# The last expert's down projection in two column halves, each scaled and scattered by itself

## The chip, the cores and the metric

The kernel runs on one core of a Trainium2 chip. The metric is the device time of one execution in microseconds (us), the median of several runs. The engines named here are PE (TensorE, matrix products), DVE (VectorE), ACT (ScalarE), POOL (GpSimd, which also issues the indirect transfers) and SP (SyncE, which issues all other transfers of this stage). Each engine takes its own instructions strictly in the order in which they stand in its queue; an instruction that waits holds up everything behind it on that engine.

## The reference, cut to what matters

The layer ends in a mixture of 16 experts. Each expert picks its 128 best tokens of 1024, computes a SwiGLU block on them and adds the result, times a gate, to the tokens' rows:

```python
gate, idx = lax.top_k(jnp.swapaxes(aff, 1, 2), cap)            # cap = 128
xg = h[bidx, idx]
hid = jax.nn.silu(xg @ w_e_gate) * (xg @ w_e_up)
y = (hid @ w_e_down) * gate[..., None]
out = jnp.zeros_like(h).at[bidx, idx].add(y)                   # then x_new + mod_l[5] * out
```

All matrices of an expert are 1024 x 1024 in float32. The 16 experts run from about 1193 us to the end.

## The kernel before, in words

A product in float32 is made of three products of shorter numbers: every operand is split into a high part (`h`, cast by ACT, line 94) and a low part (`l`, the difference, made by DVE, line 95), and `mm3` (lines 98 to 100) issues high x high, high x low and low x high into one PSUM sum. For the weights the parts are named `eh` (3 buffers) and `el` (2 buffers), each 128 x 2048, made by `split_raw` from a raw tile of 1 MB (`ma` or `me`, 15 buffers in all) that `load_raw` fetches on SP. One such pair serves 12 matmuls of 512 columns.

The order of the experts' work is `up(e)`, `gate(e + 1)`, `down(e)`. PE's order is written out by hand. The order on DVE, ACT, POOL and SP is set by a scheduler that works with estimated times when the program is built; it puts an instruction where it expects its inputs to be there. Where two instructions touch the same bytes, it adds a wait on a semaphore.

`icol` is a tile of 128 x 16 row numbers, one column for each expert. `gather(e)` reads column e to fetch the expert's tokens (`xg`), and `down(e)` reads it again for the scatter: DVE multiplies the PSUM sum by the gates into `y` (line 1311), then POOL issues an indirect transfer that adds the 128 rows of 4 KB of `y` to the output in DRAM (line 1312). Every scatter waits for the landing of the one ahead of it, since both write the output.

```python
            nc.vector.scalar_tensor_tensor(y, po, gcol[:, e:e + 1], bc5, op0=OP.mult, op1=OP.mult)
            nc.gpsimd.indirect_dma_start(out=out_rows, out_offset=bass.IndirectOffsetOnAxis(ap=icol[:, e:e + 1], axis=0),
                                         in_=y, in_offset=None, compute_op=OP.add)
```

`tsplit` transposes a 128 x 1024 tile on PE and splits it: `xgh`, `xgl` from the tokens of an expert, `hdh`, `hdl` from the hidden values (`hid`, which stands in the buffer `silu`).

Of the kernel before, what the change touches and what calls it, by code (L numbers as in the profile page):

```python
# [19 lines left out]
F32 = mybir.dt.float32  # L20
# [4 lines left out]
OP = mybir.AluOpType  # L25
AX = mybir.AxisListType

P = 128
D = 1024
KD = D // P  # L30
# [18 lines left out]
NE = 16  # L49
# [11 lines left out]
def layer_kernel(ctx: ExitStack, tc: tile.TileContext, I, rope_tab, out, dbg=None):  # L61
    nc = tc.nc
# [6 lines left out]
    x, w_in, w_ada = I["x"][0], I["w_in"][0], I["w_ada"][0]  # L69
# [27 lines left out]
    def mm3(o, lh, ll, rh, rl, start, stop):  # L97
        nc.tensor.matmul(o, lh, rh, start=start, stop=False)  # L98
        nc.tensor.matmul(o, lh, rl, start=False, stop=False)  # L99
        nc.tensor.matmul(o, ll, rh, start=False, stop=stop)  # L100
# [10 lines left out]
    def krows(w, c0, n):  # L111
        return w[:, c0:c0 + n].rearrange("(k p) n -> p k n", p=P)
# [142 lines left out]
    for m in range(2):  # L255
        for k in range(KD):
            if m == 0 or k < 4:
                nc.tensor.transpose(modv[:, m * KD + k, :], mrow[m][:, k * P:(k + 1) * P], ident[0:2, 0:2])
            else:
                for w in range(2):  # L260
# [5 lines left out]
                                   op0=OP.add, op1=OP.mult)  # L266
# [717 lines left out]
    def load_raw():  # L984

        n = len(raws)
        nm, e, k = worder[2 * n]
        pl, tg, nb = xring[n % (NME + NMA) >= NME]
        raw = pl.tile([P, 2, D], F32, name=tg, tag=tg, bufs=nb)
        nc.sync.dma_start(raw, krows(I[nm][0, e, k * P:(k + 2) * P, :], 0, D))  # L990
        raws.append(raw)

    pairs = []
# [1 line left out]
    def split_raw():  # L995
        n = len(pairs)
        while len(raws) <= n:
            load_raw()
        h = xsplit[0].tile([P, 2, D], F32R, name="eh", bufs=3)
        l = xsplit[0].tile([P, 2, D], F32R, name="el", bufs=2)  # L1000
        split(h, l, raws[n])
        pairs.append((h, l))
# [190 lines left out]
    with pool("p7a", side="right") as p7a, pool("p7", side="right") as p7:  # L1193
# [4 lines left out]
        def pq(name):  # L1198
            return ps["p"].tile([P, 1024], F32, name=name, tag="q", bufs=4)
# [91 lines left out]
        def split_hid(e):  # L1291
            HT[e] = tsplit(H.pop(e), "hd")
# [7 lines left out]
        def up(e):  # L1300
# [2 lines left out]
            nc.vector.tensor_tensor(hid, po, hid, OP.mult)  # L1303
            H[e] = hid

        def down(e):
            if e + 1 == NE:
                split_hid(e)
            po = proj("w_e_down", e, HT.pop(e))
            y = p7.tile([P, D], F32, name="y", tag="y", bufs=1)  # L1310
            nc.vector.scalar_tensor_tensor(y, po, gcol[:, e:e + 1], bc5, op0=OP.mult, op1=OP.mult)  # L1311
            nc.gpsimd.indirect_dma_start(out=out_rows, out_offset=bass.IndirectOffsetOnAxis(ap=icol[:, e:e + 1], axis=0),  # L1312
                                         in_=y, in_offset=None, compute_op=OP.add)
# [54 lines left out]
```

## Time and profile before

| | |
|---|---|
| median of 3 runs | 1768.45 us (1767.8 to 1769.65) |
| profiled execution, its own time | 1771.81 us |
| its span in the profile | 1769.8 us |
| PE busy | 1687.1 us, 95% |
| DVE busy | 1313.4 us, 74% |
| ACT busy | 1014.9 us, 57% |
| POOL busy | 264.5 us, 15% |

The shares are means over all stages. From about 1193 us on, only the experts run, and there the picture is another one; it is read from windows of one expert each. The span is the time between the first and the last instruction that the profiler recorded; the execution's own time is 2.0 us more. Every time in the rows below counts from the start of the span.

### The profile page before, as it was taken

How to read it: one execution, taken by the hardware profiler on the slowest of the kernel's cores; microseconds unless marked ns; L12 is line 12 of the kernel's file. 1: busy time of each engine (PE TensorE's matmuls, PEld its weight loads, DVE VectorE, ACT ScalarE, POOL GpSimd, SP SyncE). 2: the span in 40 equal slices, each digit the busy share in tenths (PEclk: the TensorE clock that was granted, in tenths of full speed). 3: DMA queues.
4: the chain of work that ended last, by engine and by line, in shares of the span. 5: the costliest groups of instructions: out<-in, count | busy, mean ns of one | idle time of the engine just before them, and what ended most of it. 6: DMA issues, size and time to landing. Idle time of an engine off the chain costs nothing.

```text
span 1769.8 us, 20838 instructions
## 1 busy us (share of the span) xinstructions
PE 1687.1 (95%) x7823; PEld 1356.9 (77%) x7823; DVE 1313.4 (74%) x1607; ACT 1014.9 (57%) x1105; POOL 264.5 (15%) x196
## 2 busy tenths in 40 slices
PE   8999999999999999999999999939999999999996
PEld 3788887888887877777777678827888888888885
DVE  4755456788886454787877657587999999989996
ACT  2533324876788313667776532316777777777773
POOL 1123331211221100111210100020121111112101
PEclk9999999999999999999999999969999999999999
DMA  8264444435443934000000355667999999999981
GB/s 328 100 181 101 108 121 140 131 126 167 155 144 117 318 136 152 28 28 28 29 1 1 138 199 213 234 261 286 379 395 391 403 399 381 399 402 380 389 309 24
DMA packets 174179, 363.72 MB, mean 206 GB/s; under 512 B 40160, under 2 KB 90744, under 8 KB 174080
## 3 DMA queue, kind: packets, MB, share of 16 engines
q1 hardware_dynamic: 168896, 343.54, 53.6%
q0 software_dynamic: 5184, 18.88, 4.0%
q8 instruction: 61, 1.00, 0.2%
q14 instruction: 38, 0.31, 0.0%
HBM read 314.84 MB, written 47.54 MB: 205 GB/s over the span
## 4 chain that ended last, share of the span: by engine, by line
PE 71%; DVE 11%; ACT 6%; issue 4%; DMA 4%; POOL 3%; SPq 0%; POOLq 0%; DVEq 0%; ACTq 0%
PE w_e_gate L99 3%; PE w_e_gate L100 3%; PE w_e_gate L98 3%; PE w_e_down L99 3%; PE w_e_down L100 3%; PE w_e_down L98 3%; PE w_e_up L99 3%; PE w_e_up L98 3%; PE w_e_up L100 3%; PE z L99 2%; PE z L98 2%; PE z L100 2%; PE pm L816 2%; POOL st L143 2%; PE s L98 2%
## 5 line engine op out<-in xcount | busy, mean ns | idle before, releaser
L95 DVE TENSOR_TENSOR el<-ma,eh 128x2048 fp32r<-128x2048 f32 x114 | 258.2, 2286 | 22.2 <-PE w_e_down L99 10.8
L94 ACT CAST eh<-ma 128x2048 fp32r<-128x2048 f32 x114 | 217.9, 1917 | 73.7 <-PE w_e_up L100 28.7
L95 DVE TENSOR_TENSOR el<-me,eh 128x2048 fp32r<-128x2048 f32 x78 | 176.9, 2287 | 16.6 <-ACT eh L94 6.0
L94 ACT CAST eh<-me 128x2048 fp32r<-128x2048 f32 x78 | 149.0, 1916 | 47.4 <-PE w_e_gate L100 17.3
L906 ACT ACTIVATE pr<-s 128x512 f32<-128x512 f32 x160 | 95.8, 599 | 77.2 <-PE s L100 75.8
L818 DVE TENSOR_REDUCE mx<-pm 128x1 f32<-128x320 f32 x256 | 114.4, 483 | 22.8 <-PE pm L816 20.6
L99 PE MATMUL z<-xl,wh 128*128 128x512 f32 x320 | 125.2, 392 | 1.9 <-DVE xl L280 1.9
L98 PE MATMUL z<-xh,wh 128*128 128x512 f32 x320 | 125.2, 393 | 1.0 <-DVE xh L279 0.8
L100 PE MATMUL z<-xh,wl 128*128 128x512 f32 x320 | 125.0, 391 | 1.2 <-POOL wl L326 1.2
L1312 POOL DMA_INDIRECT out_dram<-y,icol x16 | 52.3, 3268 | 469.9 <-DVE y L1311 469.9
L94 ACT CAST wh<-wr 128x1024 fp32r<-128x1024 f32 (+1 forms) x53 | 52.0, 980 | 116.1 <-PE z L99 55.0
L95 DVE TENSOR_TENSOR pl<-pr,ph 128x1024 fp32r<-128x1024 f32 x64 | 81.0, 1265 | 31.4 <-ACT ph L94 24.7
L99 PE MATMUL w_e_up<-el,xgh 128*128 128x512 f32 x256 | 100.7, 394 | 0.6 <-DVE el L95 0.6
L98 PE MATMUL w_e_gate<-eh,xgh 128*128 128x512 f32 x256 | 101.1, 395 | 0.2 <-ACT xgh L94 0.2
L99 PE MATMUL w_e_gate<-el,xgh 128*128 128x512 f32 x256 | 101.2, 395 | 0.0
L100 PE MATMUL w_e_gate<-eh,xgl 128*128 128x512 f32 x256 | 100.1, 391 | 0.8 <-DVE xgl L95 0.8
L98 PE MATMUL w_e_down<-eh,hdh 128*128 128x512 f32 x256 | 99.7, 389 | 1.1 <-ACT hdh L94 1.1
L98 PE MATMUL w_e_up<-eh,xgh 128*128 128x512 f32 x256 | 100.7, 393 | 0.0
L99 PE MATMUL w_e_down<-el,hdh 128*128 128x512 f32 x256 | 100.6, 393 | 0.0
L100 PE MATMUL w_e_down<-eh,hdl 128*128 128x512 f32 x256 | 99.9, 390 | 0.5 <-DVE hdl L95 0.5
L100 PE MATMUL w_e_up<-eh,xgl 128*128 128x512 f32 x256 | 99.8, 390 | 0.0
L816 PE MATMUL pm<-kh,qh 97*128 97x320 f32 x256 | 86.6, 353 | 7.0 <-DVE kl L95 4.1
(349 smaller groups left out, 4368.7 us busy)
## 6 DMA issues: line engine op xcount, KB each, us to landing
ma<-in_w_e_down_dram SPq DMA_DIRECT2D x40, 1024.0 KB, 9.4
ma<-in_w_e_up_dram SPq DMA_DIRECT2D x38, 1024.0 KB, 8.0
ma<-in_w_e_gate_dram SPq DMA_DIRECT2D x36, 1024.0 KB, 7.2
me<-in_w_e_gate_dram SPq DMA_DIRECT2D x28, 1024.0 KB, 7.0
me<-in_w_e_up_dram SPq DMA_DIRECT2D x26, 1024.0 KB, 8.2
me<-in_w_e_down_dram SPq DMA_DIRECT2D x24, 1024.0 KB, 9.8
wr<-in_w_in_dram SPq DMA_DIRECT2D x32, 512.0 KB, 4.5
wr<-in_w_ada_dram SPq DMA_DIRECT2D x32, 512.0 KB, 4.2
```

The source lines that it names most:

```text
L94: nc.scalar.copy(h, src)
L95: nc.vector.tensor_tensor(l, src, h.bitcast(F32), OP.subtract)
L98: nc.tensor.matmul(o, lh, rh, start=start, stop=False)
L99: nc.tensor.matmul(o, lh, rl, start=False, stop=False)
L100: nc.tensor.matmul(o, ll, rh, start=False, stop=stop)
L143: nc.gpsimd.tensor_tensor(ap, ap, h, OP.pow)
L816: nc.tensor.matmul(pm[:, 0:320], qh[:, t * P:(t + 1) * P], kh[:, g * 320:(g + 1) * 320], start=True, stop=True)
L818: nc.vector.tensor_reduce(mx[:, g, t:t + 1], pm[:, 0:320], axis=AX.X, op=OP.max)
L906: nc.scalar.activation(pr[:, sl], sp_, AF.Exp)
L1312: nc.gpsimd.indirect_dma_start(out=out_rows, out_offset=bass.IndirectOffsetOnAxis(ap=icol[:, e:e + 1], axis=0), in_=y, in_offset=None, com ...
```

## The change

The last expert (e = 15) no longer goes through `down`, but through a new `last_down`:

- its four raw tiles of `w_e_down` are fetched in another shape: 512 rows by 512 columns each (pieces of 2 KB) in place of 256 rows by 1024 columns (4 KB), so that the first two tiles hold the left half of the columns;
- PE works off the left half completely, then the right half, each into a PSUM tile of its own;
- each half is multiplied by the gates (128 x 512) and scattered by itself, into the output seen as 2048 rows of 512 columns;
- the row numbers for that (2 x row + half) are written by DVE into `icol[:, 0:1]` and `icol[:, 1:2]`, the columns of experts 0 and 1.

```diff
+        if (nm, e) == ("w_e_down", NE - 1):
+            raw4, n4 = raw.rearrange("p a (b n) -> p (a b) n", b=2), k // 2
+            nc.sync.dma_start(raw4, krows(I[nm][0, e, n4 % 2 * 512:(n4 % 2 + 1) * 512, :], n4 // 2 * 512, 512))
...
+        def last_down(e):
+            split_hid(e)
+            hh, hl = HT.pop(e)
+            halves = out_rows.rearrange("s (a n) -> (s a) n", a=2)
+            ic2 = icol
+            for n in range(2):
+                nc.vector.tensor_scalar(ic2[:, n:n + 1], icol[:, e:e + 1], 2.0, float(n), op0=OP.mult, op1=OP.add)
+            for n in range(2):
+                po = pq("w_e_down")
+                sl = slice(n * 512, (n + 1) * 512)
+                for k in range(KD):
+                    m = used[0] // 2
+                    while len(pairs) <= m + k // 4:
+                        split_raw()
+                    h, l = (x.rearrange("p a (b n) -> p (a b) n", b=2)[:, k % 4] for x in pairs[m + k // 4])
+                    mm3(po[:, sl], hh[:, k], hl[:, k], h, l, k == 0, k == KD - 1)
+                used[0] += 4
+                y = p7.tile([P, 512], F32, name="y", tag=("y", "silu")[n], bufs=1)
+                nc.vector.scalar_tensor_tensor(y, po[:, sl], gcol[:, e:e + 1], bc5[:, sl], op0=OP.mult, op1=OP.mult)
+                nc.gpsimd.indirect_dma_start(out=halves, out_offset=bass.IndirectOffsetOnAxis(ap=ic2[:, n:n + 1], axis=0),
+                                             in_=y, in_offset=None, compute_op=OP.add)
...
         def down(e):
             if e + 1 == NE:
-                split_hid(e)
+                return last_down(e)
```

Where the instructions stand shows more than the diff. DVE's queue is the first place, right behind the down projection of expert 0. A row is the line, the operation, output<-inputs and what it waits for; numbers behind a name tell tiles of one name apart, `DMASW` is a counter of POOL's transfers. Before:

```order
L1311 SCALAR_TENSOR_TENSOR y_9970<-w_e_down_9897,gcol_9500,bc5_9508 128x1024 [waits PE_49]
L95 TENSOR_TENSOR el_10026<-me_10023,eh_10025 128x2048 [waits DVE_49,DMAHW6_49,PE_49,Activation_49]
L95 TENSOR_TENSOR el_10044<-me_10041,eh_10043 128x2048 [waits DVE_49,DMAHW7_49,PE_49,Activation_49]
L95 TENSOR_TENSOR xgl_10011<-xgt_10012,xgh_10010 128x1024 [waits Activation_49]
L95 TENSOR_TENSOR el_10066<-me_10063,eh_10065 128x2048 [waits DMAHW0_49,DVE_49,PE_49]
```

and of the changed kernel, the same stretch:

```order
L1340 SCALAR_TENSOR_TENSOR y_9970<-w_e_down_9897,gcol_9500,bc5_9508 128x1024 [waits PE_49]
L95 TENSOR_TENSOR el_10026<-me_10023,eh_10025 128x2048 [waits DVE_49,DMAHW6_49,PE_49,Activation_49]
L95 TENSOR_TENSOR el_10044<-me_10041,eh_10043 128x2048 [waits DVE_49,DMAHW7_49,PE_49,Activation_49]
L1319 TENSOR_SCALAR icol_9501<-icol_9501 128x1 [waits DMASW7_49,DMASW4_49]
L95 TENSOR_TENSOR xgl_10011<-xgt_10012,xgh_10010 128x1024 [waits Activation_49]
L95 TENSOR_TENSOR el_10066<-me_10063,eh_10065 128x2048 [waits DMAHW0_49,DVE_49,PE_49]
```

The new row writes column 0 of `icol`. It stands not at the end of the program but here, two `el` tiles behind the `y` of expert 0, and waits on the counters of POOL's transfers 4 and 7. POOL's eight counters are taken in turn, and its queue shows whose they are: the gather of expert 0 has 4, and the scatter of expert 0 has 7 (the scatter of expert 1, which must wait for it, waits on `DMASW7`). The row for column 1 stands at the same place behind the `y` of expert 1 and waits on 5 and 1, the gather and the scatter of expert 1.

The second place is PE's queue at the start of the last down projection. Before, the third matmul waits for `hdl`:

```order
L98 MATMUL w_e_down_13600<-eh_13603,hdh_13587 128x512 [waits Activation_49]
L99 MATMUL w_e_down_13600<-el_13604,hdh_13587 128x512
L100 MATMUL w_e_down_13600<-eh_13603,hdl_13588 128x512 [waits DVE_49]
L98 MATMUL w_e_down_13600<-eh_13603,hdh_13587 128x512
L99 MATMUL w_e_down_13600<-el_13604,hdh_13587 128x512
```

and of the changed kernel:

```order
L98 MATMUL w_e_down_13602<-eh_13605,hdh_13587 128x512 [waits Activation_49]
L99 MATMUL w_e_down_13602<-el_13606,hdh_13587 128x512
L98 MATMUL w_e_down_13642<-eh_13645,hdh_13587 128x512 [waits PE_49]
L100 MATMUL w_e_down_13602<-eh_13605,hdl_13588 128x512 [waits DVE_49]
L98 MATMUL w_e_down_13602<-eh_13605,hdh_13587 128x512
```

One matmul of the right half (tile 13642) now stands ahead of the one that waits for `hdl`. The left half ends 23 matmuls ahead of the end of PE's queue.

The third place is the end of POOL's queue. Before, it holds the scatters of experts 14 and 15:

```order
L1312 DMA out_0_dram<-y_13510,icol_9501 1024x1024 [waits DMASW1_49,DVE_49]
L1312 DMA out_0_dram<-y_13673,icol_9501 1024x1024 [waits DMASW2_49,DVE_49]
```

and of the changed kernel:

```order
L1341 DMA out_0_dram<-y_13510,icol_9501 1024x1024 [waits DMASW1_49,DVE_49]
L1332 DMA out_0_dram<-y_13639,icol_9501 2048x512 [waits DMASW2_49,DVE_49]
L1332 DMA out_0_dram<-y_13679,icol_9501 2048x512 [waits DMASW3_49,DVE_49]
```

The last scatter has become two of half the size, and the second waits on counter 3, that of the first: it may start only when the first has landed.

## Rows read from the trace of the kernel before

**Rows 1.** Busy time by window of one expert: PE, PEld, DVE, ACT, POOL, PEclk, DMA.

```profile
1249.20:1284.00 34.80, 34.80 (x163) 28.66 (x162) 31.72 (x17) 25.91 (x16) 4.67 (x2) 1.00 1.02 387
```

**Rows 2.** Timeline of DVE behind the down projection of expert 0: start, length, instruction.

```profile
1248.43 1.28 DVE L1311 SCALAR_TENSOR_TENSOR y<-w_e_down,gcol,bc 128x1024 f32<-128x1024 f32 x1
1249.62 4.48 DVE L95 TENSOR_TENSOR el<-me,eh 128x2048 fp32r<-128x2048 f32 x2
1254.68 1.23 DVE L95 TENSOR_TENSOR xgl<-xgt,xgh 128x1024 fp32r<-128x1024 f32 x1 [0.58 <-ACT xgh L94]
1255.82 2.28 DVE L95 TENSOR_TENSOR el<-me,eh 128x2048 fp32r<-128x2048 f32 x1
```

**Rows 3.** Timeline of POOL: the scatters of experts 0, 1 and 15.

```profile
1249.99 3.41 POOL L1312 DMA_INDIRECT out_dram<-y,icol  x1 [29.86 <-DVE y L1311]
...
1284.62 3.38 POOL L1312 DMA_INDIRECT out_dram<-y,icol  x1 [29.66 <-DVE y L1311]
...
1761.38 1.55 POOL L1312 DMA_INDIRECT out_dram<-y,icol  x1 [23.95 <-DVE y L1311]
```

**Rows 4.** Line L1312, one window for each scatter: experts 0, 1, 14, 15.

```profile
DMA to landing us min/median/max: 13.1/13.1/13.1
...
DMA to landing us min/median/max: 11.6/11.6/11.6
...
DMA to landing us min/median/max: 7.7/7.7/7.7
...
DMA to landing us min/median/max: 6.1/6.1/6.1
```

**Rows 5.** Timeline of PE where the `el` tile 10066 is first used.

```profile
1257.96 0.39 PE L98 MATMUL w_e_gate<-eh,xgh 128*128 128x512 f32 x1
1258.19 0.47 PE L99 MATMUL w_e_gate<-el,xgh 128*128 128x512 f32 x1
```

**Rows 6.** Timeline of DVE behind the down projection of expert 1.

```profile
1284.26 4.48 DVE L95 TENSOR_TENSOR el<-me,eh 128x2048 fp32r<-128x2048 f32 x2
1289.32 1.23 DVE L95 TENSOR_TENSOR xgl<-xgt,xgh 128x1024 fp32r<-128x1024 f32 x1 [0.58 <-ACT xgh L94]
```

**Rows 7.** Timeline of PE after an idle time ahead of the experts.

```profile
1000.15 0.80 PE L98 MATMUL mo<-ath,wh 128*128 128x512 f32 x1 [3.08 <-DVE s L1040]
...
1001.17 0.63 PE L100 MATMUL mo<-ath,wl 128*128 128x512 f32 x1
1001.60 0.63 PE L98 MATMUL mo<-ath,wh 128*128 128x512 f32 x1
```

**Rows 8.** Windows of 1 us, same stretch; PEclk is the third value from the end.

```profile
1005.00:1006.00 1.00, 1.00 (x4) 0.79 (x3) 0.32 (x1) 0.75 (x1) 0.00 (x0) 0.50 1.02 418
1006.00:1007.00 1.00, 1.00 (x6) 0.82 (x5) 0.52 (x2) 1.00 (x3) 0.00 (x0) 0.97 1.03 418
```

**Rows 9.** Timeline of the last down projection, PE and DVE.

```profile
1748.12 0.40 PE L99 MATMUL w_e_down<-el,hdh 128*128 128x512 f32 x1
1749.05 0.50 PE L100 MATMUL w_e_down<-eh,hdl 128*128 128x512 f32 x1 [0.53 <-DVE hdl L95]
...
1754.21 2.29 DVE L95 TENSOR_TENSOR el<-ma,eh 128x2048 fp32r<-128x2048 f32 x1 [0.49 <-PE w_e_down L99]
...
1759.82 1.28 DVE L1311 SCALAR_TENSOR_TENSOR y<-w_e_down,gcol,bc 128x1024 f32<-128x1024 f32 x1 [3.32 <-PE w_e_down L100]
```

**Rows 10.** Windows of 0.5 us at the end; the last two values are DMA share, GB/s.

```profile
1763.50:1764.00 0.50, 0.00 (x0) 0.00 (x0) 0.00 (x0) 0.00 (x0) 0.00 (x0) 0.82 1.75 139
...
1766.50:1767.00 0.50, 0.00 (x0) 0.00 (x0) 0.00 (x0) 0.00 (x0) 0.00 (x0) 0.50 0.45 82
```

**Rows 11.** Groups of DVE instructions by form: count, busy us, mean ns.

```profile
L1081 DVE TENSOR_TENSOR xtmp<-xo,bc 128x512 f32<-128x512 f32 x16 | 11.0, 690 | 20.8 <-PE xo L100 20.8
L1101 DVE TENSOR_SCALAR st<-st 128x1 f32<-128x1 f32 x8 | 1.2, 153 | 5.9 <-ACT xtmp L1091 5.9
```

**Rows 12.** Timeline of SP: the last four loads. Timeline of ACT: their first use.

```profile
1701.13 8.15 SPq L990 DMA_DIRECT2D ma<-in_w_e_down_dram  x4
...
1738.87 1.92 ACT L94 CAST eh<-ma 128x2048 fp32r<-128x2048 f32 x1 [1.74 <-PE w_e_up L100]
```

More of the change, by code (lines that the diff above doesn't have):

```diff
@@ L989, in load_raw @@
         raw = pl.tile([P, 2, D], F32, name=tg, tag=tg, bufs=nb)
-        nc.sync.dma_start(raw, krows(I[nm][0, e, k * P:(k + 2) * P, :], 0, D))
+        if (nm, e) == ("w_e_down", NE - 1):
+            raw4, n4 = raw.rearrange("p a (b n) -> p (a b) n", b=2), k // 2
+            nc.sync.dma_start(raw4, krows(I[nm][0, e, n4 % 2 * 512:(n4 % 2 + 1) * 512, :], n4 // 2 * 512, 512))
+        else:
+            nc.sync.dma_start(raw, krows(I[nm][0, e, k * P:(k + 2) * P, :], 0, D))
         raws.append(raw)
```

## The prediction

> **What bounds the kernel now.** I read the windows by expert first. In the stretch of one expert PE is busy for all of its 34.80 us at full clock, DVE for 31.72 us, and the transfers fill the DMA engines (share 1.02) [rows 1]. So PE is the bound, with DVE close behind: a microsecond that PE loses here is lost for good, since there is no idle time of PE in which it could be won back. Next I read the timeline of DVE and PE together, to see how much lead DVE has. The `el` tile 10066 is made from 1255.82 to 1258.10 [rows 2], and PE starts the first matmul that reads it at 1258.19, right after the high x high matmul at 1257.96 [rows 5]. The lead is under 0.1 us, so a delay of DVE at this place is a delay of PE of the same size. Last I read the end. DVE multiplies from 1759.82 to 1761.10 [rows 9], POOL issues the scatter at 1761.38 [rows 3], and it lands 6.1 us later [rows 4], at 1767.5, of which the DMA engines move data from 1763.5 to about 1767.0 [rows 10]. The span ends at 1769.8, 2.3 us after the landing.
>
> **The change part by part.**
>
> *Column 0 of the row numbers.* The multiply itself is small: 153 ns for the nearest row, 128x1 on DVE [rows 11]. Its wait is not. It stands behind the two `el` tiles that follow the `y` of expert 0, and DVE is through with those at 1249.62 + 4.48 = 1254.10 [rows 2]. The scatter of expert 0, whose landing it waits for, is issued at 1249.99 [rows 3] and lands 13.1 us later [rows 4], at 1263.1. What is queued behind it on DVE is `xgl` and `el` 10066. With some 0.2 us for the wake-up and the multiply, `xgl` starts at 1263.3 in place of 1254.68: 8.6 us late, and so is `el` 10066. PE waits for it with nothing else ahead in its hand-written order: **8.6 us**. The scatter cannot land much sooner because of the stall: its rivals on the DMA engines are loads that were issued before 1254.1, and that is also when the stall begins. I bound this term at 8.0 and 8.9.
>
> *Column 1.* The same at expert 1, moved back by what was lost so far. Before, the scatter is issued at 1284.62 [rows 3] and `xgl` starts at 1289.32 [rows 6], 4.70 later. If the scatter needs L from issue to landing, DVE and PE lose L + 0.2 - 4.7. For L the rows give 11.6 (this scatter as it was) and 7.7 (that of expert 14, with no loads beside it) [rows 4], so the loss lies between 3.2 and 7.1. The stall before has stopped the loads for 8.6 us, since SP may only load into a raw tile that DVE is done with, so the queue in front of this scatter is shorter; but two loads are released by the `el` tiles just behind the `y` and run beside it. That is nearer to the first row. I take L = 10.5: **6.0 us**.
>
> *The clock of PE behind each stall.* The trace has no idle time of PE among the experts that is this long, so I go by one ahead of them. After 3.08 us of idling PE resumes at 1000.15, and its matmuls of 512 columns start 0.43 us apart (1001.17, 1001.60) [rows 7], where they stand 0.23 us apart among the experts [rows 5]; the granted clock is 0.50 up to 1006 and 0.97 in the microsecond behind it [rows 8]. That is 1.2 GHz in place of 2.4 for 5.9 us after the idle time, some 14 matmuls at 0.2 us too much: 2.8 us. Both stalls here are longer than 3.08 us or about as long. The bounds are nothing (the clock stays, or the slow matmuls only use up time that DVE needs anyway) and 2.8. DVE needs 2.2 us for a tile and PE at the low clock 12 x 0.43 = 5.1, so DVE gives no cover; I take **2.7 us each**, 5.4 in all.
>
> *The matmul that moves up.* At the last down projection PE starts a matmul at 1748.12 and the next only at 1749.05, since `hdl` is late [rows 9]. One matmul of the right half goes into that gap. It gains **0.2 us**.
>
> *The end.* The left half is complete 23 matmuls ahead of the end, but on DVE its multiply stands behind the last `el` tile, which ends at 1756.50 [rows 9]. It takes about 0.69 us, the nearest row with 512 columns from PSUM [rows 11], in place of 1.28. The first scatter can be issued 0.28 us after that, as at the end now (1761.10 to 1761.38): at 1757.5. For its landing the bounds are 6.1 us (as many rows as the whole one) and 4.4 us (the 3.5 us of data halved) [rows 4, 10]. The second scatter waits for that landing, until 1762.2 to 1763.9 with the 0.28 us, although its own `y` is ready by 1760.3; it lands again 4.4 to 6.1 us later, at 1766.6 to 1770.0, where the one whole scatter lands at 1767.5. So the end moves by -0.9 to +2.5 us. Half the bytes should be nearer to the lower price; with 5.0 us for each it is **+0.3 us**, the matmul above included, which is hidden then. The chain at the end has one more transfer in series, and that uses up what the halves save.
>
> *The rest.* The four loads in the new shape are issued between 1701.1 and 1709.3 and first cast at 1738.87 [rows 12]. Even with the 13.1 us of the slowest scatter they would be there by 1722.4, so smaller pieces cost nothing; a load later than 29 us would show. Count and size of matmuls and splits do not change. The raw tiles lie 15 deep, so the loads that the stalls hold back are still early.
>
> Sum in the profiled execution: 8.6 + 2.7 + 6.0 + 2.7 + 0.3 = 20.3 us on its own time of 1771.81. The stalls are differences within one execution, so the same 20.3 us go on the median of 1768.45, 3.4 us lower: **1788.8 us**, 1.1% slower. Less than 0.2% (3.5 us) is what a measurement of this kernel can hardly tell from no change.
>
> **A rule against this.** The rows of this kernel give 6.1 to 13.1 us for a scatter, and the stall rests on that. The Trainium skill (DMA: Bandwidth & Descriptors, section "Anatomy of one DMA — SWDGE (gpsimd) path") states some 2.0 us plus bytes / 436 GB/s for a transfer issued by POOL. That would be an estimate of 3.2 us for 512 KB, by which the scatter would land at 1253.2, ahead of DVE's arrival at 1254.10, and both stalls would be gone. The trace does not agree: even with all else silent it shows 6.1 us.
>
> **The rivals.**
>
> - *The waits are already met when DVE gets there* (not slower). It takes a scatter that lands within 4.1 us of its issue (1254.10 - 1249.99), or a wait on something older than that scatter. Against it: the four landings of [rows 4], all above 6, and the order of POOL's counters. For it: only that waits of this kind are cheap elsewhere. Then the end alone is left: 1768.45 + 0.3 = 1768.8, between 1767.5 and 1771. The rule above gives the same time. Chance 0.06.
> - *Stalls without the clock.* PE idles, but its clock stays or comes back at once. Against it are [rows 7, 8]; for it, that the idle time there was in another stage. 8.6 + 6.0 + 0.3 = 14.9: 1783.4. Chance 0.13.
> - *More than two stalls' worth.* DVE has 3 us of reserve in 34.8 [rows 1]; if late tiles meet further late tiles (the next `hdl`, `y` and gather all shift too), a few us come on top, or L at expert 1 is above 11.6. About 1796. Chance 0.06.
> - *Forecast as summed*, between 1781 and 1793. Chance 0.75.
>
> **How the numbers follow.** Lower end of the forecast's own terms: 8.0 + 0 + 3.2 + 0 - 0.9 = 10.3, which is 1778.8; upper end 8.9 + 2.8 + 7.1 + 2.8 + 2.5 = 24.1, which is 1792.6. All bounds at one end together are unlikely; the range 1780 to 1793.5 takes in the forecast and the rival without the clock, nearly 9 in 10. Slower by over 0.2% are all cases but the first: 0.93 with a little taken off for what I overlooked; within 0.2%: 0.06; faster: 0.01, since a gain above 3.5 us has no place to come from: the whole way from the last matmul to the end is 10 us.
>
> **What the profile of the changed kernel would show.** Right: DVE idle for about 9 us near 1254 and for 3 to 7 us some 46 us later, ended by the multiply of `icol` with a transfer to the output as releaser; PE idle for as long, with a granted clock of 0.50 behind it; the scatter of expert 1 landing after 8 to 12 us; and at the end two scatters, the second issued only after the first has landed. Wrong: no idle time of DVE there; a stall of DVE that PE doesn't follow; a landing at the end more than 1 us earlier in distance from the last matmul than the 7.7 us of now. The prediction fails most easily on L at expert 1 and on the clock.

## The result, and the profile after

The changed kernel takes 1790.5 us in the median of 5 runs (1785.61 to 1792.77), beside 1767.8 us (1766.53 to 1769.65) for the kernel before: a ratio of 1.0107, with a 95% interval of 1.0091 to 1.0123. The medians are 22.7 us apart; the ratio would be 18.9 us on 1767.8 (16.1 to 21.7), so the size is known to a few us only. 1788.8 us was predicted, between 1780 and 1793.5. The profiled span is 1788.8 us, beside 1769.8, 19.0 us more. This profiled execution came to the scatter of expert 0 3.2 us sooner than the one before (1246.76 us against 1249.99, rows below and [rows 3]), for no reason that the change gives: in the 14 profiled executions of this document that time lies between 1246.8 and 1253.4. From that scatter to the end of the span it is 542.0 us, beside 519.8, and these 22.2 us are what has to be explained.

First the timeline of DVE in the changed kernel, behind the down projections of experts 0 and 1 (start, length, instruction, and in brackets the idle time ahead of it with what ended it):

```profile
1246.39 4.48 DVE L95 TENSOR_TENSOR el<-me,eh 128x2048 fp32r<-128x2048 f32 x2
1260.46 0.15 DVE L1319 TENSOR_SCALAR icol<-icol 128x1 int32<-128x1 int32 x1 [9.58 <-DMA out_dram<-y,icol]
1260.53 1.22 DVE L95 TENSOR_TENSOR xgl<-xgt,xgh 128x1024 fp32r<-128x1024 f32 x1
...
1292.90 4.48 DVE L95 TENSOR_TENSOR el<-me,eh 128x2048 fp32r<-128x2048 f32 x2
1305.00 0.15 DVE L1319 TENSOR_SCALAR icol<-icol 128x1 int32<-128x1 int32 x1 [7.62 <-DMA out_dram<-y,icol]
1305.07 1.22 DVE L95 TENSOR_TENSOR xgl<-xgt,xgh 128x1024 fp32r<-128x1024 f32 x1
```

Each of the two small writes takes 0.15 us and is preceded by 9.58 and 7.62 us in which DVE does nothing, and the releaser is a transfer to the output that reads `icol`. From the start of the pair of `el` tiles to `xgl` it is now 14.14 and 12.17 us; before, it was 5.06 both times (1249.62 to 1254.68 in [rows 2], 1284.26 to 1289.32 in [rows 6]). So `xgl`, and all that stands behind it on DVE, comes 9.08 and 7.11 us late.

PE in the same kernel, same places:

```profile
1254.73 0.39 PE L98 MATMUL w_e_gate<-eh,xgh 128*128 128x512 f32 x1
1264.00 0.79 PE L99 MATMUL w_e_gate<-el,xgh 128*128 128x512 f32 x1 [8.88 <-DVE el L95]
1264.59 0.63 PE L100 MATMUL w_e_gate<-eh,xgl 128*128 128x512 f32 x1
1265.02 0.63 PE L98 MATMUL w_e_gate<-eh,xgh 128*128 128x512 f32 x1
...
1308.54 0.80 PE L99 MATMUL w_e_gate<-el,xgh 128*128 128x512 f32 x1 [6.91 <-DVE el L95]
```

These answer to [rows 5]: the high x high matmul runs, and the next one waits for the late `el`. Behind the wait matmuls start 0.43 us apart (1264.59, 1265.02). The windows of the stretch show why (length, busy time of PE, PEld, DVE, ACT, POOL, then granted clock, DMA share, GB/s):

```profile
1260.00:1264.00 4.00, 0.00 (x1) 0.01 (x1) 3.54 (x4) 0.00 (x0) 0.00 (x0) 0.50 0.27 112
1264.00:1269.90 5.90, 5.90 (x14) 4.64 (x15) 4.46 (x3) 0.76 (x1) 0.00 (x0) 0.50 0.80 290
1270.10:1275.00 4.90, 4.90 (x27) 4.13 (x26) 3.21 (x2) 3.60 (x3) 0.00 (x0) 1.00 0.72 254
```

PE does 14 matmuls in 5.9 us at a granted clock of 0.50 (1.2 GHz of 2.4) and 27 in 4.9 us at 1.00.

In the slow stretch a matmul starts 0.2 us later behind the one ahead of it than the 0.23 us of the full clock [rows 5]; 14 of them make 2.8 us.

How much an expert took in all is read from POOL's scatters in the changed kernel:

```profile
1246.76 3.41 POOL L1341 DMA_INDIRECT out_dram<-y,icol  x1 [29.87 <-DVE y L1340]
...
1293.27 3.38 POOL L1341 DMA_INDIRECT out_dram<-y,icol  x1 [41.53 <-DVE y L1340]
...
1337.71 3.38 POOL L1341 DMA_INDIRECT out_dram<-y,icol  x1 [39.48 <-DVE y L1340]
```

The distances are 46.51 and 44.44 us, where the kernel before has 34.63 ([rows 3], and the same again for the next expert): 11.88 and 9.81 us lost. All the later distances but those of the last expert are the old ones to within 0.05 us. The landings of the first two and of the two halves at the end (line L1341 with a window for each scatter, then line L1332):

```profile
DMA to landing us min/median/max: 13.6/13.6/13.6
...
DMA to landing us min/median/max: 11.7/11.7/11.7
...
DMA to landing us min/median/max: 4.8/4.9/4.9
```

And the end of the changed kernel, first PE where it goes on after the wait for the last `hdl`, then DVE's last `el` tile and two multiplies, then POOL's two scatters:

```profile
1767.53 0.50 PE L100 MATMUL w_e_down<-eh,hdl 128*128 128x512 f32 x1 [0.30 <-DVE hdl L95]
...
1772.69 2.29 DVE L95 TENSOR_TENSOR el<-ma,eh 128x2048 fp32r<-128x2048 f32 x1 [0.49 <-PE w_e_down L99]
1774.90 0.75 DVE L1331 SCALAR_TENSOR_TENSOR y<-w_e_down,gcol,bc 128x512 f32<-128x512 f32 x1
...
1775.92 1.55 POOL L1332 DMA_INDIRECT out_dram<-y,icol  x1 [20.01 <-DVE y L1331]
...
1778.08 0.75 DVE L1331 SCALAR_TENSOR_TENSOR y<-w_e_down,gcol,bc 128x512 f32<-128x512 f32 x1 [2.43 <-PE w_e_down L100]
...
1781.59 1.55 POOL L1332 DMA_INDIRECT out_dram<-y,icol  x1 [4.11 <-DMA out_dram<-y,icol]
```

The second scatter goes out 3.51 us after its multiply began, since it waits for the first one's landing. From the last multiply's start to the end of the span it is 10.7 us; before it was 10.0 (1759.82 in [rows 9], 1769.8): 0.7 us longer. From the wait for `hdl` to the last multiply it is 10.55 us and was 10.77 ([rows 9]): 0.22 us shorter, by the matmul that moved into the gap, and the wait itself fell from 0.53 to 0.30. From PE's going on (1767.53, before 1749.05) to the end of the span it is 21.27 us and was 20.75: 0.52 us longer in all.

### The profile page after: what moved, and what is told of

Read it like the earlier page. It is cut to its first block, busy times and chain, and to the rows that moved or that the text cites. A ratio compares the mean times of both kernels' runs of the same rounds, so it can differ in the third digit from the quotient of the medians.

```text
span 1788.8 us, 20843 instructions
## 1 busy us (share of the span) xinstructions
PE 1694.6 (95%) x7823; PEld 1363.0 (76%) x7823; DVE 1313.6 (73%) x1610; ACT 1014.8 (57%) x1105; POOL 265.8 (15%) x197
## 4 chain that ended last, share of the span: by engine, by line
PE 66%; DVE 11%; issue 8%; ACT 6%; DMA 5%; POOL 3%; SPq 0%; POOLq 0%; DVEq 0%; ACTq 0%
PE w_e_gate L99 3%; PE w_e_down L99 3%; PE w_e_down L100 3%; PE w_e_down L98 3%; PE w_e_gate L100 3%; PE w_e_gate L98 3%; PE w_e_up L99 3%; PE w_e_up L98 3%; PE w_e_up L100 3%; POOL st L143 2%; PE z L99 2%; PE z L100 2%; PE z L98 2%; PE pm L816 2%; PE s L98 2%
## 5 line engine op out<-in xcount | busy, mean ns | idle before, releaser
L95 DVE TENSOR_TENSOR el<-ma,eh 128x2048 fp32r<-128x2048 f32 x114 | 258.4, 2287 | 24.9 <-PE w_e_down L99 10.8
L95 DVE TENSOR_TENSOR el<-me,eh 128x2048 fp32r<-128x2048 f32 x78 | 177.1, 2287 | 18.9 <-PE w_e_gate L99 5.8
L99 PE MATMUL z<-xl,wh 128*128 128x512 f32 x320 | 126.4, 396 | 0.8 <-DVE xl L280 0.8
L1341 POOL DMA_INDIRECT out_dram<-y,icol x15 | 50.7, 3381 | 467.6 <-DVE y L1340 467.6
L99 PE MATMUL w_e_gate<-el,xgh 128*128 128x512 f32 x256 | 103.7, 405 | 15.8 <-DVE el L95 15.8
L95 DVE TENSOR_TENSOR pl<-pr,ph 128x1024 fp32r<-128x1024 f32 x64 | 81.0, 1265 | 31.5 <-ACT ph L94 24.7
L99 PE MATMUL w_e_up<-el,xgh 128*128 128x512 f32 x256 | 100.8, 394 | 0.6 <-DVE el L95 0.6
L99 PE MATMUL w_e_down<-el,hdh 128*128 128x512 f32 x256 | 100.6, 393 | 0.0
```

The costliest lines, as they stand in the source:

```text
L95: nc.vector.tensor_tensor(l, src, h.bitcast(F32), OP.subtract)
```

## The experiments

The theory: DVE's two early writes wait for two landings, PE waits for DVE with no cover and comes back at the low clock, and that is all of the loss; the halves themselves cost next to nothing. The rivals: the loss sits in the halves (other loads, other order on PE, another end), or PE's wait is all and the clock adds nothing.

**Row numbers in a tile of their own** (e1_own_tile).

```diff
-            ic2 = icol
+            ic2 = p7.tile([P, 2], I32, name="ic2")
```

> The changed kernel with one edit: the two columns of row numbers stand in a small tile of their own, no longer in columns 0 and 1 of icol. Theory (the two multiplies make DVE wait for the scatters of experts 0 and 1, and PE waits for DVE): no wait of DVE on a transfer, the distances between the scatters of experts 0, 1 and 2 are back at 34.6 us each, and only the difference at the end is left (+0.7 us behind the last matmul, -0.2 us ahead of it): 1768.3 us against 1767.8 before. Rival (the time is lost in the last expert's own work: loads in small pieces, two PSUM tiles, two scatters): nothing changes, about 1790.

Measured: 1781.96 us (1780.6 to 1789.81) beside 1773.02 (1768.36 to 1778.79) for the kernel before, which is the time to compare with here and in the next three experiments; ratio 1.0057 (1.004 to 1.0074). DVE goes on to `xgl` without the wait:

```profile
1254.56 1.23 DVE L95 TENSOR_TENSOR xgl<-xgt,xgh 128x1024 fp32r<-128x1024 f32 x1 [0.74 <-ACT xgh L94]
```

No wait of DVE on a transfer is left among the experts, so the stalls are gone; but the kernel is still 9 to 10 us slower than before, since the distances between the scatters of experts 0 to 14 are now 35.33 to 35.45 in place of 34.63 to 34.88 (one, between experts 9 and 10, is 33.66 and was 33.04). PE is busy all through, at full clock (35.00 of 35.00 us from 1285 to 1320, granted clock 1.00). The time that the theory gave was missed, and something was added that it doesn't know; experiments further down take it up.

**The two writes alone** (e2_writes_alone): the kernel before, whole last projection and whole scatter, with nothing but the two writes put in.

```diff
+                for n in range(2):
+                    nc.vector.tensor_scalar(icol[:, n:n + 1], icol[:, e:e + 1], 2.0, float(n), op0=OP.mult, op1=OP.add)
```

> The kernel before, with nothing but the two multiplies into columns 0 and 1 of icol added at the last expert; nobody reads what they write. Theory: both stalls as in the changed kernel, DVE idle 9.6 and 7.6 us on the transfers, PE idle 8.9 and 6.9 us, 5.9 us of low clock behind each: 21.7 us on the time before, 1789.5. Rival (the last expert's own work): as before, 1767.8 to 1768.5.

Measured: 1791.23 us (1790.11 to 1794.71), ratio 1.0101 (1.0071 to 1.013), which overlaps that of the whole change. The timeline of DVE and of POOL:

```profile
1248.93 4.49 DVE L95 TENSOR_TENSOR el<-me,eh 128x2048 fp32r<-128x2048 f32 x2
1261.22 0.15 DVE L1310 TENSOR_SCALAR icol<-icol 128x1 int32<-128x1 int32 x1 [7.80 <-DMA out_dram<-y,icol]
1261.29 1.22 DVE L95 TENSOR_TENSOR xgl<-xgt,xgh 128x1024 fp32r<-128x1024 f32 x1
...
1249.30 3.41 POOL L1314 DMA_INDIRECT out_dram<-y,icol  x1 [29.86 <-DVE y L1313]
...
1292.81 3.38 POOL L1314 DMA_INDIRECT out_dram<-y,icol  x1 [38.53 <-DVE y L1313]
```

The writes without any halves make the same two stalls (7.80 us here, 7.22 at expert 1). The two distances are 8.88 and 8.94 us above 34.63 (11.88 and 9.81 in the changed kernel), and the measured time can't be told from that of the whole change. The rival that puts the loss into the halves falls.

**One column of the old row numbers** (e3_one_column): the left half's numbers in `icol[:, 0:1]`, the right half's in a new tile.

```diff
+            ic3 = p7.tile([P, 2], I32, name="ic3")
...
-                nc.vector.tensor_scalar(ic2[:, n:n + 1], icol[:, e:e + 1], 2.0, float(n), op0=OP.mult, op1=OP.add)
+                nc.vector.tensor_scalar((ic2, ic3)[n][:, n:n + 1], icol[:, e:e + 1], 2.0, float(n), op0=OP.mult, op1=OP.add)
```

> The changed kernel, but only the left half's row numbers go into column 0 of icol; the right half's go into a tile of their own. Theory: the first stall alone is left, 8.9 us of idling and 3.0 us of low clock, the distance from the scatter of expert 1 to that of expert 2 is back at 34.6 us: 1767.8 + 11.9 + 0.5 = 1780.2. If the second stall were only an echo of the first (the loads that were held back), it would stay although its multiply is gone, and the time would be about 1790.

Measured: 1792.33 us (1790.18 to 1794.19), ratio 1.0105 (1.0077 to 1.0133). DVE waits once, 9.04 us at expert 0; the distance there is 45.92 and the next one 35.34, so the second stall went with the second column. The time was missed again: the other distances are 35.33 to 35.44 (33.66 between experts 9 and 10), as with the own tile, which costs the 10 us again that the second stall no longer costs.

**PE kept busy in the stalls** (e4_pe_filled): the changed kernel with 36 and 28 matmuls whose result nobody reads (the first matmul of the gate overwrites it), ahead of the gate projections of experts 2 and 3, behind which PE would wait.

```diff
+        FILL = {2: 36, 3: 28}
...
+                if nm == "w_e_gate" and k == 0:
+                    for _ in range(FILL.get(e, 0)):
+                        nc.tensor.matmul(po[:, 0:512], op_[0][:, 0], h[:, 0:512], start=True, stop=True)
```

> The changed kernel with 36 and 28 matmuls without use (their result is overwritten) put on PE ahead of the gate projections of experts 2 and 3, where PE idles for 8.9 and 6.9 us; at 0.227 us they fill 8.2 and 6.3 us of it. Theory (behind each stall the low clock of PE costs 2.8 to 3.0 us): the granted clock stays at 1.00, the distances between the scatters fall from 46.5 and 44.5 to about 43.5 and 41.6 us, 1784.7 in all. Rival (the time behind the idling is lost because DVE's tiles come late, whatever PE's clock): distances and time stay, 1790.5.

Measured: 1788.06 us (1786.65 to 1793.23), ratio 1.0087 (1.0056 to 1.0119). One window:

```profile
1260.00:1264.00 4.00, 4.00 (x19) 3.34 (x18) 1.06 (x2) 0.00 (x0) 0.00 (x0) 1.00 0.97 353
```

and the timelines of PE, DVE and POOL:

```profile
1257.71 8.32 PE L1292 MATMUL w_e_gate<-eh,xgh 128*128 128x512 f32 x36
...
1249.37 4.49 DVE L95 TENSOR_TENSOR el<-me,eh 128x2048 fp32r<-128x2048 f32 x2
1262.94 0.15 DVE L1324 TENSOR_SCALAR icol<-icol 128x1 int32<-128x1 int32 x1 [9.08 <-DMA out_dram<-y,icol]
1263.01 1.21 DVE L95 TENSOR_TENSOR xgl<-xgt,xgh 128x1024 fp32r<-128x1024 f32 x1
...
1249.74 3.41 POOL L1346 DMA_INDIRECT out_dram<-y,icol  x1 [29.84 <-DVE y L1345]
...
1292.97 3.38 POOL L1346 DMA_INDIRECT out_dram<-y,icol  x1 [38.26 <-DVE y L1345]
```

The clock stays at 1.00. `xgl` is late by 1263.01 - 1249.37 - 5.06 = 8.58 us, and the distance to the next scatter is 43.23, 8.60 above 34.63: with the clock kept, the loss is DVE's delay and nothing more (6.44 us on both sides at expert 1). In the changed kernel the same sums leave 11.88 - 9.08 = 2.80 and 9.81 - 7.11 = 2.70 us, and that is the low clock. The rival without the clock falls by these distances; the measured times alone don't decide it, since the ratio of the changed kernel, 1.0107, lies within the interval of this one.

**Row numbers in an old tile that nobody reads any more** (f1_mask_tile): no new tile, so nothing moves.

```diff
-            ic2 = icol
+            ic2 = msk.bitcast(I32)
```

> The changed kernel with the two products written into columns of the old mask tile, which no transfer reads any more, in place of the row-number columns that the scatters of experts 0 and 1 read; no tile is added, so no address moves. Theory (the two stalls and the low clock behind them are all of the loss among the experts): no wait of the vector engine on an output transfer, distances between scatters 34.6 us throughout as in the kernel before, matmuls 0.227 us apart, and only the end differs: last transpose to last matmul 0.23 us shorter, last matmul to the end of the span 0.69 us longer, +0.46 us in all, a ratio of 1.0003 (1768.3 where the kernel before takes 1767.8). Rival (the loss sits in the column halves, wherever the row numbers stand): still about 20 us slower. Second rival (what slowed every matmul with the own tile was the other place of the row numbers, not the moved addresses): distances of 35.35 us here too, some 11 us slower.

Measured: 1774.05 us (1769.83 to 1776.03) beside 1771.94 (1768.13 to 1778.58) for the kernel before, which is the time to compare with in the next two experiments and in f3_shift_alone too; ratio 0.9999 (0.9988 to 1.0011). The medians are 2.1 us apart, less than the spread of either kernel. POOL's timeline and DVE's last multiply:

```profile
1251.54 3.41 POOL L1341 DMA_INDIRECT out_dram<-y,icol  x1 [29.86 <-DVE y L1340]
...
1286.17 3.38 POOL L1341 DMA_INDIRECT out_dram<-y,icol  x1 [29.66 <-DVE y L1340]
...
1761.26 0.75 DVE L1331 SCALAR_TENSOR_TENSOR y<-w_e_down,gcol,bc 128x512 f32<-128x512 f32 x1 [2.43 <-PE w_e_down L100]
```

The distance is 34.63 again, and so are the others up to expert 9 to within 0.02; the last multiply begins at 1761.26 and the span ends 10.7 us later. From the scatter of expert 0 to the end of the span (1772.0) it is 520.5 us, 0.7 more than the 519.8 of the kernel before, where 0.46 was expected. With the two writes out of the way, the halves take as long as the whole to within what the runs can tell. The 21.7 us lost between the scatters were the place of the row numbers.

**The left half into another tensor** (f2_first_half_elsewhere): as the kernel with the mask tile, but the left half's scatter adds into `h2_d` (`h_d` in the rows). It leaves out the left half of the last expert's contribution to the output.

```diff
+            h2_halves = h2_d.rearrange("s (a n) -> (s a) n", a=2)
...
-                nc.gpsimd.indirect_dma_start(out=halves, ...
+                nc.gpsimd.indirect_dma_start(out=(h2_halves, halves)[n], ...
```

> As the kernel with the mask tile, but the left half's scatter adds into another DRAM tensor (the gathered rows' source) and not into the output, so the left half of the last expert's contribution is left out of the output; the second scatter then has no earlier scatter of the same tensor in flight. Theory (the second scatter waits for the landing of the first, 4.11 us after its data were there, [4.11 <-DMA out_dram] in the changed kernel): it goes out about 2.2 to 2.6 us after the last product's start and not 3.5, the time from last matmul to the end of the span comes down from 10.7 to 7.2 to 8.5 us, and the whole is 2.2 to 3.5 us under the kernel with the mask tile. Rival (the two scatters' descriptors and bytes pass one queue and POOL anyway, so the order costs the same): no change, 10.7 us.

Measured: 1771.51 us (1766.75 to 1774.02), ratio 0.9992 (0.9981 to 1.0004), an interval that overlaps that of the kernel with the mask tile; the profile tells more. The timelines of POOL and DVE:

```profile
1761.34 1.55 POOL L1333 DMA_INDIRECT h_d<-y,msk  x1 [22.29 <-DVE y L1332]
1764.52 1.55 POOL L1333 DMA_INDIRECT out_dram<-y,msk  x1 [1.63 <-DVE y L1332]
...
1763.49 0.75 DVE L1332 SCALAR_TENSOR_TENSOR y<-w_e_down,gcol,bc 128x512 f32<-128x512 f32 x1 [2.43 <-PE w_e_down L100]
```

The second scatter now follows the start of its multiply by 1.03 us in place of 3.5 (2.2 to 2.6 were expected), and from there to the end of the span (1771.8) it is 8.3 us in place of 10.7. So it is the wait for the first landing that eats what the halves save at the end. The program sets that wait because both scatters write the output tensor. The two halves add to different columns of it, so their sums don't ask for it; whether the program could do without it was not tried.

**Halves with one scatter** (e6_one_scatter): both halves multiplied into one `y`, one scatter of whole rows with the old row numbers, no write to `icol`.

```diff
+            y = p7.tile([P, D], F32, name="y", tag="y", bufs=1)
...
+                nc.vector.scalar_tensor_tensor(y[:, sl], po[:, sl], gcol[:, e:e + 1], bc5[:, sl], op0=OP.mult, op1=OP.mult)
+            nc.gpsimd.indirect_dma_start(out=out_rows, out_offset=bass.IndirectOffsetOnAxis(ap=icol[:, e:e + 1], axis=0),
+                                         in_=y, in_offset=None, compute_op=OP.add)
```

> The last down projection by column halves, each with its own PSUM tile and its own multiply, but one scatter of whole rows with the old row numbers; nothing is written into the row-number columns. Theory: no stalls among the experts (distances as in the kernel before); in the last expert the matmul that moved up gives 0.23 us, and the multiply behind the last matmul is a half (0.75 us in the changed kernel) instead of a whole (1.28 us before), 0.53 us; in all about -0.76 us against the kernel before, a ratio of 0.9996, less than a measurement tells from no change. Rival (the halves themselves cost something that the stalls hid): slower than the kernel before by over 1 us.

Measured: 1771.52 us (1768.47 to 1775.52), ratio 0.9997 (0.9985 to 1.0009). The last multiply and the scatter:

```profile
1760.38 0.75 DVE L1326 SCALAR_TENSOR_TENSOR y<-w_e_down,gcol,bc 128x512 f32<-128x512 f32 x1 [2.43 <-PE w_e_down L100]
...
1761.40 1.55 POOL L1327 DMA_INDIRECT out_dram<-y,icol  x1 [23.21 <-DVE y L1326]
```

From the multiply's start to the end of the span (1769.8) it is 9.4 us, 0.6 less than before, and from the scatter of expert 0 (1250.66) to the end it is 519.1 us, 0.7 less. The profile shows the gain that was expected, and the runs can't tell it from nothing. By the profile this is the best form of the change found that computes the whole output, and it doesn't measurably beat the kernel before.

**What the own tile cost.** The kernels with a new tile of 8 bytes have the same instructions as others without it, but in the allocation of the compiled kernel the tiles `hdh`, `hdl`, `xgh` and `xgl`, which PE loads as weights of its matmuls, begin 32 bytes lower in each partition. So do `bc5`, `y`, `silu` and `xg`; the weights' tiles `eh` and `el` stay. The traces show no addresses. f3_shift_alone puts an unused tile of 8 bytes into the kernel before, ahead of the experts:

```diff
         bc5 = p7.tile([P, D], F32, name="bc5")
+        nc.vector.memset(p7.tile([P, 2], I32, name="shift"), 0)
```

> The kernel before with nothing but an unused tile of 8 bytes per partition in the pool of the experts' tiles, set once to zero ahead of the experts; no instruction of the experts is changed. Theory (the moved addresses of the tiles that the matmuls read and the vector engine writes slow each matmul): distances between scatters 35.35 us and not 34.63, matmuls 0.234 us apart and not 0.227, +10 to +11 us in all, a ratio of 1.006. Rival (the row numbers in their own tile cost it in the kernel with the own tile, by another order of instructions): distances of 34.63 and no change of the time.

Measured: 1771.77 us (1769.43 to 1774.94), ratio 0.9996 (0.9984 to 1.0008), distances of 34.63: no loss. But in this place the new tile moved `bc5` alone, and not what the matmuls read, so it tells nothing against the addresses. g1_hid_moved puts it where `hdh` and `hdl` move, and `xgh` and `xgl` don't:

```diff
         def split_xg(e):
+            if e == 0:
+                nc.vector.memset(p7.tile([P, 2], I32, name="shift"), 0)
```

> The kernel before with an unused tile of 8 bytes per partition put between the tiles of the gathered rows and their split halves, so that the split halves of the hidden rows (hdh, hdl, the weights that down's matmuls load) begin 32 bytes lower in each partition and those of the gathered rows (xgh, xgl, gate and up) stay. The unused tile ahead of all of them moved bc5 alone and cost nothing; the row numbers' own tile moved hdh, hdl, xgh and xgl by 32 bytes and cost 0.71 us for each expert. Theory (what counts is where a matmul's loaded operand begins): down's 48 matmuls for each expert slow from 0.227 to about 0.232 us apart, gate's and up's stay; distances between scatters 34.87 us (a third of 0.71 more than 34.63), +3.8 us in all. Rival (the row numbers' own tile costs by something else, such as who waits for whom, not by addresses): distances of 34.63 and no change. Second rival (the tiles that the vector and scalar engines write are what counts): slower by another share, with all matmuls alike.

Measured: 1780.04 us (1777.67 to 1784.66) beside 1772.36 (1768.95 to 1775.84) for the kernel before, which is the time to compare with from here on; ratio 1.0054 (1.0034 to 1.0073), distances of 34.89 to 34.92. The distances are those of the theory, the time isn't: they make 4.0 us from expert 0 to expert 14, and 7.7 us were measured. In the profiled execution another 1.9 us lie in the last expert (29.16 us between the last two scatters, before 27.31), where the granted clock was 0.50 from 1753.8 to 1756.8; where the rest lies is not shown, with four runs 7 us apart. g2_own_64 and g3_own_128 are the changed kernel with an own tile of 64 and of 128 bytes:

```diff
-            ic2 = icol
+            ic2 = p7.tile([P, 16], I32, name="ic2")
```

(in the second, `[P, 32]`.)

> The changed kernel with the row numbers in their own tile, which is 64 bytes per partition (of which 8 are used), so that hdh, hdl, xgh and xgl begin 64 bytes lower than in the kernel before and not 32 as with the 8-byte tile. Theory (a loaded operand that begins at a multiple of 64 bytes is as fast as before): distances 34.63 us, the time that of the kernel with the mask tile, a ratio of 1.000. Rival (only multiples of 128 bytes are): distances of about 35.35, +11 us, a ratio of 1.006.

> The same with 128 bytes per partition: the instructions are those of the kernel with the 8-byte own tile, one for one, and hdh, hdl, xgh and xgl begin 128 bytes lower than in the kernel before. Theory (the 11 us of the 8-byte tile were the shift of addresses alone): distances 34.63 us, matmuls 0.227 us apart, end +0.46 us, a ratio of 1.0003. Rival (a tile of their own costs by itself, or the shift does at any size): distances 35.35, a ratio of 1.006.

Measured: 1776.24 us (1770.99 to 1779.23), ratio 1.0022 (1.0011 to 1.0033), distances of 34.82 to 34.84 up to expert 9; and 1781.32 us (1778.07 to 1784.12), ratio 1.0046 (1.0031 to 1.006), distances of 35.19 to 35.29. The groups of PE's matmuls between 1400 and 1560 us, one of down and one of up in each kernel (count, busy us, mean ns), show where the time went. The kernel before:

```profile
L98 PE MATMUL w_e_down<-eh,hdh 128*128 128x512 f32 x80 | 31.1, 389 | 0.0
...
L100 PE MATMUL w_e_up<-eh,xgl 128*128 128x512 f32 x67 | 26.1, 389 | 0.0
```

with the own tile of 8 bytes (the weights of both moved by 32 bytes):

```profile
L98 PE MATMUL w_e_down<-eh,hdh 128*128 128x512 f32 x75 | 29.6, 395 | 0.0
...
L100 PE MATMUL w_e_up<-eh,xgl 128*128 128x512 f32 x64 | 25.3, 395 | 0.0
```

with `hdh` and `hdl` moved by 32 bytes, and `xgh` and `xgl` not:

```profile
L98 PE MATMUL w_e_down<-eh,hdh 128*128 128x512 f32 x80 | 31.6, 395 | 0.0
...
L100 PE MATMUL w_e_up<-eh,xgl 128*128 128x512 f32 x64 | 24.9, 390 | 0.0
```

with all four moved by 64 bytes:

```profile
L98 PE MATMUL w_e_down<-eh,hdh 128*128 128x512 f32 x80 | 31.4, 392 | 0.0
...
L100 PE MATMUL w_e_up<-eh,xgl 128*128 128x512 f32 x64 | 25.1, 392 | 0.0
```

and by 128 bytes:

```profile
L98 PE MATMUL w_e_down<-eh,hdh 128*128 128x512 f32 x71 | 28.0, 395 | 0.0
...
L100 PE MATMUL w_e_up<-eh,xgl 128*128 128x512 f32 x68 | 26.8, 394 | 0.0
```

Within one kernel the groups differ by up to 6 ns (the before's L99 of down has 394), so a group is compared with the same group of another kernel. Where down's weights moved and those of gate and up didn't, down's matmuls are slower, 395 ns against 389, and up's are not (390). `bc5`, `y`, `silu` and `xg` moved there too, just as with the own tile of 8 bytes; of all these tiles only `xgh` and `xgl` lie in different places in these two kernels, and up's matmuls take 390 and 395 ns. So it is the place of what a matmul loads that counts; that accounts for the distances with the own tile and with the single column. The other half of the theory fell: 128 bytes are as bad as 32 (nearly), and 64 bytes cost 3 ns where nothing was expected. Which places are good isn't known from four of them; that stays open.

**The writes made late** (e5_late_rows): columns 0 and 1 of `icol` as in the change, but with an addend worked out from the last expert's hidden values (times 0.0), so that DVE gets to them only at the end.

```diff
-                nc.vector.tensor_scalar(ic2[:, n:n + 1], icol[:, e:e + 1], 2.0, float(n), op0=OP.mult, op1=OP.add)
+                late = p7.tile([P, 1], F32, name="late", bufs=2)
+                nc.vector.tensor_scalar(late, hid15[:, 0:1], 0.0, float(n), op0=OP.mult, op1=OP.add)
+                nc.vector.tensor_scalar(ic2[:, n:n + 1], icol[:, e:e + 1], 2.0, late, op0=OP.mult, op1=OP.add)
```

> The changed kernel with its columns of the old row numbers, but the two writes get an addend worked out from the last expert's hidden rows (times 0.0, so the numbers are the same), and the vector engine can reach them only when that is there, at the end. Theory (the columns are harmless once the scatters of experts 0 and 1 have landed, the loss is that the writes were put early): no wait of the vector engine on an output transfer, distances 34.63 us if no tile is moved and 35.35 if the small tile of the addend moves the matmuls' operands by 32 bytes; the end +0.5 to +1.5 us, since two or three small instructions stand in the vector engine's queue there; ratio 1.000 to 1.001 without the shift. Rival (the wait costs wherever the writes stand): still a wait of several us on an output transfer, some 10 us slower.

Measured: 1774.44 us (1772.78 to 1779.05) beside 1772.36 (1768.95 to 1775.84) for the kernel before, ratio 1.0012 (1.0001 to 1.0023). No wait on a transfer is left among the experts, so the columns as such are harmless: it was when they are written. The distances up to expert 9 are 34.80 to 34.84, as with the tile of 64 bytes; in the allocation the two small tiles moved the weights by 64 bytes here too.

## Why the prediction was right

Term by term, as the prediction made its sum:

| term | predicted | measured in the changed kernel |
|---|---|---|
| stall at expert 0 | 8.6 us (8.0 to 8.9) | 9.1, `xgl` late |
| clock behind it | 2.7 (0 to 2.8) | 2.8, the rest of the 11.88 (14 matmuls at 0.2) |
| stall at expert 1 | 6.0 (3.2 to 7.1) | 7.1 |
| clock behind it | 2.7 | 2.7, the rest of the 9.81 |
| the end, matmul moved up included | +0.3 (-0.9 to +2.5) | +0.5 (21.27 us, before 20.75) |
| sum | 20.3 | 22.2 (in the medians 22.7, by the ratio 18.9) |

- *The stalls.* The mechanism held: two columns, two landings, two waits of DVE, and PE behind them with no lead; the kernel with the two writes alone repeats it, and the kernels with the mask tile and with late writes have none of it. Mis-sized was the landing time L. At expert 1 the prediction took 10.5 us, since the stall ahead would shorten the queue of loads, and it was 11.7; that is 1.1 of the 1.9 us that the sum is short. The stall ahead shortens L by less than that: in the four profiled executions with a stall at expert 0, L at expert 1 is 11.0 to 11.7, in the ten without 11.5 to 12.4. At expert 0 the scatter took 13.6 and not 13.1 us, which makes another 0.5 and puts the term 0.2 above its upper bound: the bound had taken one execution's 13.1 as nearly fixed. It isn't: over the 14 profiled executions L at expert 0 is 11.7 to 14.5, and with the writes alone (11.8) the term comes to 7.3, below its lower bound. The bounds of 8.0 and 8.9 were too narrow to both sides, and that 13.1 came so near to the 13.6 of the changed kernel is in part luck. In seven stalls of four kernels (the changed one, the writes alone, PE kept busy, one column) DVE's idle time is L less 4.0 to 4.1 us: 13.6 and 9.58, 11.7 and 7.62, 11.8 and 7.80, 11.3 and 7.22, 13.1 and 9.08, 11.0 and 6.95, 13.1 and 9.04. So the uncertainty of a stall sits in L.
- *The clock.* The prediction carried a price over from an idle time of 3.08 us in another stage [rows 7, 8], and it fits to 0.1 us here. That is in part luck, since it isn't a constant: in the kernel with the writes alone the same sums leave 8.88 - 7.30 = 1.6 us at expert 0 (`xgl` late by 1261.29 - 1248.93 - 5.06, distance 43.51), where the slow matmuls last for 3.5 us (1264.76 to 1268.24) and not for 5.9, and 2.2 us at expert 1 (distance 43.57); both lie within the bounds.
- *The end.* Two transfers in series were seen rightly; each lands 4.8 to 4.9 us after its issue (5.0 taken), and the second waits 4.11 us for the first. The matmul's 0.2 us was called hidden, and it is: it brings the last multiply 0.22 us nearer, but the second scatter doesn't wait for that. It waits for the first landing, and the first multiply stands behind the last `el` tile, which starts 5.16 us after PE goes on, as it did before (1767.53 to 1772.69; 1749.05 to 1754.21 in [rows 9]).
- *The rule by which the waits would have been met.* The Trainium skill (DMA: Bandwidth & Descriptors, section "Anatomy of one DMA — SWDGE (gpsimd) path") gives 2.0 us and bytes / 436 GB/s, an estimate of 3.2 us for a whole scatter and 2.6 us for a half. The trace doesn't agree: 13.6 and 11.7 us beside the loads, 4.8 us for a half with no load beside it. The measurement decides.
- *An error in the description.* The section on the kernel says that PE's order is written out by hand, and the prediction repeats it at the first stall. That is so ahead of the experts, down to the selection of their tokens; among the experts the scheduler sets PE's order as well, and it was the scheduler that moved the matmul of the right half up. The sum doesn't hang on it, since `el` was next in PE's queue either way ([8.88 <-DVE el L95]).

## What to carry to other kernels

A write into an old tile waits for the transfers that still read the same bytes (here the gather and the scatter of the expert whose column it was), and an engine that works in order holds up all that stands behind the write: before reusing a few bytes, look where in the engine's queue the write comes to stand and which landing it waits for, or take bytes that nobody reads any more. In a stretch that PE bounds, such a wait cost the delay of DVE (6.7 to 9.1 us in the four stalls of the changed kernel and of the writes alone) and 1.6 to 2.8 us of low clock on top. And a new tile, however small, moves others: compare the mean duration of the matmuls before and after, group by group, since up to 6 ns on each were about 10 us here.

## What the runs showed that was not expected

- A matmul of 128x512 took, in the two groups shown, 389, 392 or 395 ns depending on where in the partition its loaded operand begins (0, 64, 32 bytes lower; at 128 it was 394 to 395). Among the 16 experts, with 144 such matmuls each, that is about 10 us, nearly half as much as the stalls.
- In 5 of the 14 profiled executions the clock was low at the start of the last down projection, behind the waits of 1.3 and 1.1 us around the last transposes, and in 9 it was not. The kernel with the mask tile and the one with the left half elsewhere have the same instructions there. Windows of the first:

```profile
1749.00:1755.00 6.00, 5.25 (x22) 4.04 (x23) 3.53 (x3) 2.08 (x2) 0.00 (x0) 1.00 0.00 0
```

and of the second:

```profile
1749.00:1755.00 6.00, 5.60 (x13) 4.35 (x14) 1.65 (x3) 0.35 (x1) 0.00 (x0) 0.50 0.00 0
```

22 matmuls against 13 in the same 6 us. From the start of the last transposes to the last multiply it is 14.0 us in the one (1747.26 to 1761.26) and 16.3 in the other (1747.21 to 1763.49), which is why the spans of the two are alike (1772.0 and 1771.8) though the second's end is 2.4 us shorter. A difference of 2 us between two profiled executions can be this alone.
